# A hybrid encoder on one core: a q projection that ends token tile by token tile, gatings set apart, gate logits turned by full tiles

## The chip, the core and the metric

The kernel runs on one core of one Trainium2 chip. The metric is the device time of one execution in microseconds, of which the median of several runs is given. The engines named here are TensorE (PE; its weight loads are shown apart as PEld), VectorE (DVE), ScalarE (ACT), GpSimd (POOL) and SyncE (SP). Each takes its instructions in order. SyncE only issues DMAs here; GpSimd issues some too.

## The reference

Two layers, 256 tokens, model width 1024, everything in fp32. One input projection feeds two branches: a gated delta rule in both directions (in chunks of 64 tokens, after a convolution of width 5) and a differential softmax attention with partial rotary. Both have a SiLU gate path; they are merged with sigmoid gates.

```python
for l in range(DEPTH):
    h = rmsnorm(x, norm_w[l])
    proj = h @ w_in[l]
    (q_a, k_a, v_a, ab_a, z_a, q_b, k_b, v_b, z_b,
     gate_a, gate_b) = jnp.split(proj, SPLIT_IDX, axis=-1)
    y_a = gated_delta_branch(q_a, k_a, v_a, ab_a, z_a, conv_w[l], a_log[l], ...)
    lambda_init = 0.8 - 0.6 * math.exp(-0.3 * l)
    y_b = diff_attention_branch(q_b, k_b, v_b, z_b, cos, sin, diff_lambda[l], ...)
    merged = (jax.nn.sigmoid(gate_a) * (y_a @ w_pa[l])
              + jax.nn.sigmoid(gate_b) * (y_b @ w_pb[l]))
    x = x + merged @ w_out[l]
return rmsnorm(x, final_norm_w)
```

`ab_a` has 32 columns per token, the logits of the delta rule's gates. The attention's output is gated by the line `return o * jax.nn.silu(z)` at the end of its branch, `o` being a root-mean-square norm per head.

## The kernel before

**Tiles and products.** The 256 tokens are two token tiles of 128 (`m` = 0 and 1, NM = 2), the inner dimension is eight tiles of 128 (`kt`, KT = 8). Weights come from memory in pieces of 512 KB (`raw`, two inner tiles by 512 columns, called a `kp`), which ScalarE rounds to the upper part (`hi`, L308) and VectorE subtracts to the lower part (`lo`, L310). Each product is made of three: hi by hi, lo by hi, hi by lo (L324 to L326 in `proj_tm`, which accumulates one PSUM bank of 128 tokens by 512 columns for each token tile; L385 to L389 in the function for the convolution, with tiles pf_q, pf_k, pf_v and 256 columns). In a row of the profile lo_ga is then the lower part of a piece of the a gate's weights (`C_GA`, two halves of 512 columns, "ga0" and "ga1"), pp_ga its product; the b gate, gb, goes ahead of it. The rows leave out buffer numbers, so both token tiles' banks have one name there.

**What sets the order.** The program is written in the order of the data flow; a scheduler that simulates a time line decides each engine's order from it, from priorities, and from places written by hand: `behind(ins)` lets an instruction be issued only behind another one. `mark[name, kp]` keeps the instructions that made the upper and the lower part of a piece, so "after the lower part of ga0's third piece" is `mark["ga00", 2][1]` in the first layer. PSUM has eight banks in three pools; projections (pp, pf) take theirs in turn from one of four.

**The first place: q projection to v convolution.** The rotated attention's q comes in two halves; the second is "qk01" (evac_qk: ScalarE copies a token tile's bank to `stg`, L597, VectorE rotates, TensorE transposes). The first accumulator of the v convolution, pf_v, takes over the bank that token tile 0 of this projection leaves.

**The second: gate logits.** Their product abp has 64 rows: 32 columns of weights, upper and lower parts. It is copied to abT (64 x 256) and turned to tokens by rows by two products with id2, a 64 x 32 matrix of two identities above each other, which also adds the two parts (L636); VectorE copies the result to ab. Transposes of full tiles against the identity stand elsewhere, as ctk (L706). gcps (L764) is the first product that needs the logits.

**The third: gatings of the attention output.** For head half `i` and token tile `m`, VectorE multiplies the four heads by their factor and by the SiLU path (L1197, four instructions, ob), and transposes in blocks of 32 (L249, zb); GpSimd issues a DMA of 256 KB to a bounce buffer in memory (bny_yb, L251) and four DMAs of 64 KB that fetch it back turned (L257). `split_B` then makes the upper part on ScalarE (ybT, L263) and the lower one on VectorE (L265), for the product with w_pb. Around this stand the last steps of the delta rule's triangular inverse (`merges`, `join`): T, transposed blocks (L954); y128p and zt (L961); y1p and sp (L992), between which ScalarE copies A (L1000) and ktm (L1006); TensorE works through pp_ga between them. tb_q are squares for a norm of q (L135, L1046, L1047).

```python
at = [mark[f"ga{l}0", 1 + m][1] if i else mark[f"gb{l}1", 2 + m][1] for m in range(NM)]
```

This line of `gate_yb(i)` places the four gatings: half 0 behind the lower parts of the b gate's last two pieces, half 1 behind those of the a gate's second and third pieces.

Of the kernel before, what the change touches and what calls it, by code (L numbers as in the profile page):

```python
# [8 lines left out]
F32 = mybir.dt.float32  # L9
# [3 lines left out]
ALU = mybir.AluOpType  # L13
# [4 lines left out]
P = 128  # L18
DM = 1024
KT = DM // P  # L20
SEQ = 256
NM = SEQ // P
# [27 lines left out]
def hybrid_encoder(  # L50
# [44 lines left out]
    def bank_c(name):  # L95
        return ps_c.tile([P, 512], F32, tag="c", name=name)
# [4 lines left out]
    def last(ap, n):  # L101
        return ap.unsqueeze(ap.ndim).to_broadcast(list(ap.shape) + [n])

    mark = {}
# [4 lines left out]
    G.memset(ident, 1.0)  # L109
    G.affine_select(out=ident, in_=ident, compare_op=ALU.is_equal, fill=0.0,  # L110
                    base=0, pattern=[[1, P]], channel_multiplier=-1)
    id2 = const.tile([64, 32], F32, name="id2")
    V.tensor_tensor(id2, ident[0:64, 0:32], ident[0:64, 32:64], ALU.add)
    G.memset(tri, 1.0)
    for d, sg in ((0, 1), (1, -1)):
        G.affine_select(out=tri[:, d, :], in_=tri[:, d, :], compare_op=ALU.is_ge,
# [137 lines left out]
    def fetch(tb, dd, after):  # L254
        for j in range(4):
            with behind(after):
                G.dma_start(out=tb[blk(j)], in_=dd[:, :, j].rearrange("i t x -> t i x"))  # L257
# [55 lines left out]
                yield 2 * kp + k, hi[:, k, :n], lo[:, k, :n]  # L313

    def proj_tm(act, w, c0, n, evac, nm, places=(None,) * 4, spare=(), later=None, turned=(), between=None,
                banks=None, held=None, first=(), raws={}):

        accs = (banks or banks2)(f"pp_{nm}")
        for kt, hi, lo in weights(w, c0, n, nm, places, later=later, spare=spare, turned=turned, held=held,
                                  first=first, raws=raws):  # L320
            for m in range(NM):
                ts_ = slice(m * P, (m + 1) * P)
                o = accs[m][:, :n]
                T.matmul(o, act[kt // 4][:, 0, kt % 4, ts_], hi, start=kt == 0, stop=False)  # L324
                T.matmul(o, act[kt // 4][:, 0, kt % 4, ts_], lo, start=False, stop=False)  # L325
                mark["proj"] = T.matmul(o, act[kt // 4][:, 1, kt % 4, ts_], hi, start=False,  # L326
                                        stop=kt == KT - 1).ins
                mark["done", nm, kt] = mark["proj"]
        if between:
            between()  # L330
        for m in range(NM):
            evac(m, accs[m][:, :n])
# [174 lines left out]
    for l in range(DEPTH):  # L507
# [86 lines left out]
        def qk_part(s_, i):  # L594
                def evac_qk(m, ps):
                    st = work.tile([P, 512], F32, tag="w2a", name=f"stg{l}{s_}{i}{m}", bufs=2)
                    S.copy(st, ps)  # L597
                    g_ = st.rearrange("p (g e) -> p g e", e=DH)
                    x12 = g_[:, :, 0 : 2 * RD].rearrange("p g (x r) -> p g x r", x=2)
                    both = lambda t_: mid(mid(t_[:, m, :], 2), 8)  # L600
                    r4 = small.tile([P, 2, 8, 2, RD], F32, tag="r4", name=f"r4{l}{s_}{i}{m}", bufs=1)
                    V.tensor_tensor(r4[:, 0], x12, both(cos), ALU.mult)
                    V.tensor_tensor(r4[:, 1], x12, both(sin), ALU.mult)
                    V.tensor_tensor(x12[:, :, 0], r4[:, 0, :, 0], r4[:, 1, :, 1], ALU.subtract)
                    V.tensor_tensor(x12[:, :, 1], r4[:, 0, :, 1], r4[:, 1, :, 0], ALU.add)
                    pt = bank(f"qkt{l}{m}{s_}{i}")
                    for b in range(4):
                        T.transpose(pt[:, b * P : (b + 1) * P], st[:, b * P : (b + 1) * P], ident)

                    mark["qkT", m] = S.mul(qkT[i][:, s_, :, m * P : (m + 1) * P],  # L610
                                           pt.rearrange("p (b t) -> p b t", b=4), (DH ** -0.5, 1.0)[s_]).ins
                proj_tm(hT, wl, (C_QB, C_KB)[s_] + 512 * i, 512, evac_qk, f"qk{l}{s_}{i}",
                        turned=(0, 1) if (s_, i) == (0, 1) else ())

# [11 lines left out]
        for kt in range(KT):  # L628
            for part in range(2):
                T.matmul(abp[0:64, :SEQ], wabr[:, kt, :], hT[kt // 4][:, part, kt % 4, :],  # L630
                         start=kt == 0 and part == 0, stop=kt == KT - 1 and part == 1)
        abT = work.tile([64, SEQ], F32, tag="w2c", name=f"abT{l}", bufs=3)
        mark["ab"] = S.copy(abT, abp[0:64, :SEQ]).ins
        abq = bank_c(f"abq{l}")
        for m in range(NM):
            T.matmul(abq[:, m * 32 : (m + 1) * 32], abT[:, m * P : (m + 1) * P], id2,  # L636
                     start=True, stop=True)
        V.tensor_copy(ab.rearrange("p m c -> p (m c)"), abq[:, :64])

        a_ = small.tile([P, NM, 32], F32, tag="ga_", name=f"ga_{l}")  # L640
        V.tensor_scalar(a_[:, :, 0:16], ab[:, :, 0:16], -1.0, None, ALU.mult)
# [603 lines left out]
        V.scalar_tensor_tensor(rb, rb, 0.5 * (1.0 - lam0), r0, ALU.mult, ALU.mult)  # L1245

        ybT, yb_sent = pair(f"ybT{l}"), {}
        def gate_yb(i):
            at = [mark[f"ga{l}0", 1 + m][1] if i else mark[f"gb{l}1", 2 + m][1] for m in range(NM)]
            gated(lambda i, m: heads4(ob[i][:, m, :]), zb, rb, nw[:, 1:2], ybT, f"yb{l}",  # L1250
                  after={(i, m): at[m] for m in range(NM)}, halves_=(i,), sent=yb_sent)
            for m in range(NM):
                fetch(*yb_sent[i, m], None)

        gate_yb(0)
        gta = gate(C_GA, f"ga{l}", "eo", (lambda: gate_yb(1), None))
        for i, m in ((0, 0), (0, 1), (1, 0), (1, 1)):
            split_B(ybT[i], yb_sent[i, m][0], m, nw[:, 1:2], mark[f"ga{l}{i}", 2 + m])
        branch(ybT, w_pb[l], gtb, f"pb{l}")
# [137 lines left out]
```

## Time and profile before

| | |
|---|---|
| median of 3 runs | 743.0 us (742.79 to 744.36) |
| the profiled execution | 742.73 us |
| its span in the trace | 740.8 us |
| granted TensorE clock, mean | 0.997 of full |
| moved by DMA | 135.43 MB, mean 183 GB/s |

A row of the time line has the start and the length in microseconds, the engine, the line, the operation, the tiles it writes and reads, their shapes, and how many like instructions are taken together; in brackets stands how long the engine was idle ahead of it and what ended that. Matmuls are pipelined, so their lengths overlap, and the step from one start to the next is what one costs. A row of the view of waits has the engine and line that waited, what for, the sum in microseconds, the number of times and the longest. An fp32 product or transpose takes two passes and is counted twice.

### The profile page before, as it was taken

Reading aid. Unit: us, or ns where it says so; the run is one execution under the profiler, and the core shown is the slowest. Engines: PE = TensorE matmul, PEld = TensorE weight load, DVE = VectorE, ACT = ScalarE, POOL = GpSimd, SP = SyncE. Lnnn points to the kernel's source line nnn. Section 1 sums busy time; section 2 is a strip of 40 time slices with the busy share of each in tenths; the row PEclk is TensorE's granted clock in tenths of the full one; section 3 lists DMA queues with packets and bytes.
Section 4 is the critical chain, followed back from the end, with each engine's and each line's share of the span. In section 5 each row is a group of like instructions: output and inputs, shape, how many; then the busy total and the mean of one; then the engine's idle time right before and its main releaser. Section 6 shows DMA issues by size and latency. Waiting matters only on the chain.

```text
span 740.8 us, 13649 instructions
## 1 busy us (share of the span) xinstructions
PE 732.1 (99%) x5034; PEld 635.6 (86%) x5034; DVE 588.5 (79%) x1119; ACT 479.5 (65%) x1018; POOL 140.9 (19%) x223
## 2 busy tenths in 40 slices
PE   9999999999999999999999999999999999999996
PEld 6999889987888899888889899889788888998885
DVE  8696898999986885578667769999999769728782
ACT  6666875667876586645456578555787748665552
POOL 6004110112022433100000150202110514311000
PEclk9999999999999999999999999999999999999998
DMA  8755667776766473567674466767766736436641
GB/s 264 239 173 171 172 181 195 209 207 203 208 181 163 136 208 104 173 205 246 201 234 138 129 192 184 212 175 236 200 173 197 203 116 196 150 124 204 213 142 57
DMA packets 73732, 135.43 MB, mean 183 GB/s; under 512 B 12912, under 2 KB 13921, under 8 KB 73666
## 3 DMA queue, kind: packets, MB, share of 16 engines
q1 hardware_dynamic: 64750, 113.65, 51.6%
q0 software_dynamic: 7936, 19.35, 9.1%
q10 hardware_dynamic: 980, 1.58, 0.6%
q8 instruction: 39, 0.64, 0.4%
q14 instruction: 27, 0.22, 0.1%
HBM read 125.53 MB, written 9.01 MB: 182 GB/s over the span
## 4 chain that ended last, share of the span: by engine, by line
PE 96%; ACT 2%; issue 1%; DVE 1%; POOLq 0%; POOL 0%; DVEq 0%; ACTq 0%
PE pp_vb L369 4%; PE pp_qk L325 4%; PE pp_qk L326 3%; PE pp_qk L324 3%; PE sc L1067 2%; PE pp_o L369 2%; PE pp_za L325 2%; PE pf_k L385 2%; PE pf_v L385 2%; PE pf_v L389 2%; PE pp_ga L324 2%; PE pp_gb L324 2%; PE pp_zb L324 2%; PE pf_q L387 2%; PE pf_k L389 2%; PE pf_k L387 2%
## 5 line engine op out<-in xcount | busy, mean ns | idle before, releaser
L325 PE MATMUL pp_qk<-lo_qk,hT 128*128 128x512 f32 x128 | 50.5, 394 | 0.3
L326 PE MATMUL pp_qk<-hi_qk,hT 128*128 128x512 f32 x128 | 49.9, 390 | 0.0
L310 DVE TENSOR_TENSOR lo_qk<-raw_qk,hi_qk 128x1024 fp32r<-128x1024 f32 x32 | 39.1, 1221 | 12.0 <-ACT hi_qk L308 11.7
L324 PE MATMUL pp_qk<-hi_qk,hT 128*128 128x512 f32 x128 | 45.1, 393 | 0.0
L308 ACT CAST hi_qk<-raw_qk 128x1024 fp32r<-128x1024 f32 x28 | 29.4, 1049 | 23.4 <-PE pp_qk L326 12.7
L1077 ACT ACTIVATE es<-sc,mx 128x256 f32<-128x256 f32 x64 | 29.6, 473 | 19.5 <-DVE mx L1075 19.5
L385 PE MATMUL pf_q<-hT,hi_q 128*128 128x256 f32 x128 | 36.1, 285 | 0.0
L387 PE MATMUL pf_q<-hT,hi_q 128*128 128x256 f32 x128 | 35.9, 284 | 0.0
L385 PE MATMUL pf_k<-hT,hi_k 128*128 128x256 f32 x128 | 35.9, 286 | 0.0
L387 PE MATMUL pf_k<-hT,hi_k 128*128 128x256 f32 x128 | 35.9, 285 | 0.0
L385 PE MATMUL pf_v<-hT,hi_v 128*128 128x256 f32 x128 | 35.8, 285 | 0.0
L387 PE MATMUL pf_v<-hT,hi_v 128*128 128x256 f32 x128 | 35.8, 284 | 0.0
L389 PE MATMUL pf_q<-hT,lo_q 128*128 128x256 f32 x128 | 35.2, 288 | 0.0
L310 DVE TENSOR_TENSOR lo_pb<-raw_pb,hi_pb 128x1024 fp32r<-128x1024 f32 x16 | 19.6, 1225 | 18.9 <-ACT hi_pb L308 18.9
L389 PE MATMUL pf_v<-hT,lo_v 128*128 128x256 f32 x128 | 34.6, 288 | 0.0
L389 PE MATMUL pf_k<-hT,lo_k 128*128 128x256 f32 x128 | 34.3, 284 | 0.0
L308 ACT CAST hi_pa<-raw_pa 128x1024 fp32r<-128x1024 f32 x16 | 16.9, 1055 | 22.2 <-PE pp_pa L326 16.1
L679 DVE SCALAR_TENSOR_TENSOR cvq<-pf_q,cw,cvq 128x254 f32<-128x254 f32 (+1 forms) x64 | 30.0, 479 | 0.9 <-ACT cvq L675 0.4
L679 DVE SCALAR_TENSOR_TENSOR cvv<-pf_v,cw,cvv 128x254 f32<-128x254 f32 (+1 forms) x64 | 29.9, 479 | 0.1
L325 PEld LDWEIGHTS pp_qk<-lo_qk,hT 128*128 128x128 f32 x128 | 24.0, 188 | 6.6 <-DVE lo_qk L310 1.6
L679 DVE SCALAR_TENSOR_TENSOR cvk<-pf_k,cw,cvk 128x254 f32<-128x254 f32 (+1 forms) x64 | 28.5, 476 | 1.5 <-ACT cvk L675 0.9
L310 DVE TENSOR_TENSOR lo_pa<-raw_pa,hi_pa 128x1024 fp32r<-128x1024 f32 x16 | 19.6, 1224 | 11.2 <-ACT hi_pa L308 11.2
(416 smaller groups left out, 2535.1 us busy)
## 6 DMA issues: line engine op xcount, KB each, us to landing
raw_qk<-in_w_in_dram SPq DMA_DIRECT2D x32, 512.0 KB, 3.8
raw_k<-in_w_in_dram SPq DMA_DIRECT2D x16, 512.0 KB, 4.6
raw_q<-in_w_in_dram SPq DMA_DIRECT2D x16, 512.0 KB, 3.7
raw_v<-in_w_in_dram SPq DMA_DIRECT2D x16, 512.0 KB, 3.8
raw_zb<-in_w_in_dram SPq DMA_DIRECT2D x16, 512.0 KB, 4.0
raw_za<-in_w_in_dram SPq DMA_DIRECT2D x16, 512.0 KB, 3.8
raw_ga<-in_w_in_dram SPq DMA_DIRECT2D x16, 512.0 KB, 4.6
raw_pb<-in_w_pb_dram SPq DMA_DIRECT2D x16, 512.0 KB, 4.0
```

Of the source, the lines that this page charges most:

```text
L308: high = (V.tensor_copy if kp in turned else S.copy)(hi[:, :, :n], raw[:, :, :n]).ins
L310: mark[nm, kp] = high, V.tensor_tensor(lo[:, :, :n], raw[:, :, :n], hi[:, :, :n].bitcast(F32), ALU.subtract).ins
L324: T.matmul(o, act[kt // 4][:, 0, kt % 4, ts_], hi, start=kt == 0, stop=False)
L325: T.matmul(o, act[kt // 4][:, 0, kt % 4, ts_], lo, start=False, stop=False)
L326: mark["proj"] = T.matmul(o, act[kt // 4][:, 1, kt % 4, ts_], hi, start=False, stop=kt == KT - 1).ins
L369: mark["proj"] = T.matmul(o, act[kt // 4][:, pa, kt % 4, ts_], ws[kt][1 + pw], start=kt == 0 and n_ == 0, stop=kt == KT - 1 and n_ == 2).ins
L385: T.matmul(o, hi[:, cs], act[kt // 4][:, 0, kt % 4, :], start=first, stop=False, skip_group_check=True)
L387: T.matmul(o, hi[:, cs], act[kt // 4][:, 1, kt % 4, :], start=False, stop=False, skip_group_check=True)
L389: T.matmul(o, lo[:, cs], act[kt // 4][:, 0, kt % 4, :], start=False, stop=done, skip_group_check=True)
L679: V.scalar_tensor_tensor(ca[:, o0:o1], acc[:, b, o0 + sft : o1 + sft], cw[:, j, cb : cb + 1], ca[:, o0:o1], ALU.mult, ALU.add)
L1067: mm = T.matmul(sp[n][:, qt * SEQ : (qt + 1) * SEQ], qkT[h // 4][rows, 0, h % 4, qt * P : (qt + 1) * P], qkT[h // 4][rows, 1, h % 4, :], s ...
L1077: S.activation(es[:, n, qt, :], spv[:, qt, :], AF.Exp, bias=mx[:, n, qt : qt + 1], accum_out=s_all[:, h, n, qt : qt + 1])
```

## The change

Three edits. (1) `proj_tm` gets `by_tile`, used for "qk01" alone: the last two inner tiles are not multiplied as they come but held until both are there, and then first for token tile 0, then for token tile 1. (2) abT gets 128 rows, whose lower half GpSimd clears; the two products with id2 become two transposes of full 128x128 tiles, and VectorE adds the two halves behind its copy; id2 goes. (3) Each gating of the attention output has a place of its own: (0, 0) as before, (0, 1) behind the lower part of ga0's first piece, (1, 0) behind that of the third, (1, 1) behind that of the fourth. The places of the splits are not changed.

```diff
     def proj_tm(act, w, c0, n, evac, nm, places=(None,) * 4, spare=(), later=None, turned=(), between=None,
-                banks=None, held=None, first=(), raws={}):
+                banks=None, held=None, first=(), raws={}, by_tile=False):
 
         accs = (banks or banks2)(f"pp_{nm}")
+        ws = {}
         for kt, hi, lo in weights(w, c0, n, nm, places, later=later, spare=spare, turned=turned, held=held,
                                   first=first, raws=raws):
-            for m in range(NM):
+            ws[kt] = hi, lo
+            if by_tile and kt == KT - 2:
+                continue
+            todo = [(m, k) for m in range(NM) for k in ((kt - 1, kt) if by_tile and kt == KT - 1 else (kt,))]
+            for m, k in todo:
...
-                        turned=(0, 1) if (s_, i) == (0, 1) else ())
+                        turned=(0, 1) if (s_, i) == (0, 1) else (), by_tile=(s_, i) == (0, 1))
...
-        abT = work.tile([64, SEQ], F32, tag="w2c", name=f"abT{l}", bufs=3)
-        mark["ab"] = S.copy(abT, abp[0:64, :SEQ]).ins
-        abq = bank_c(f"abq{l}")
+        abT = work.tile([P, SEQ], F32, tag="w2c", name=f"abT{l}", bufs=3)
+        G.memset(abT[64:P], 0.0)
+        mark["ab"] = S.copy(abT[0:64], abp[0:64, :SEQ]).ins
+        abq = bank_c(f"abq{l}")[:, :SEQ].rearrange("p (m c) -> p m c", m=NM)
         for m in range(NM):
-            T.matmul(abq[:, m * 32 : (m + 1) * 32], abT[:, m * P : (m + 1) * P], id2,
-                     start=True, stop=True)
-        V.tensor_copy(ab.rearrange("p m c -> p (m c)"), abq[:, :64])
+            T.transpose(abq[:, m, :], abT[:, m * P : (m + 1) * P], ident)
+        V.tensor_copy(ab, abq[:, :, 0:32])
+        V.tensor_tensor(ab, ab, abq[:, :, 32:64], ALU.add)
...
-        def gate_yb(i):
-            at = [mark[f"ga{l}0", 1 + m][1] if i else mark[f"gb{l}1", 2 + m][1] for m in range(NM)]
+        def gate_yb(i, m, at):
             gated(lambda i, m: heads4(ob[i][:, m, :]), zb, rb, nw[:, 1:2], ybT, f"yb{l}",
-                  after={(i, m): at[m] for m in range(NM)}, halves_=(i,), sent=yb_sent)
-            for m in range(NM):
-                fetch(*yb_sent[i, m], None)
-
-        gate_yb(0)
-        gta = gate(C_GA, f"ga{l}", "eo", (lambda: gate_yb(1), None))
+                  (m,), {(i, m): at}, (i,), yb_sent)
+            fetch(*yb_sent[i, m], None)
+
+        def gate_others():
+            for i, m, kp, part in ((0, 1, 0, 1), (1, 0, 2, 1), (1, 1, 3, 1)):
+                gate_yb(i, m, mark[f"ga{l}0", kp][part])
+
+        gate_yb(0, 0, mark[f"gb{l}1", 2][1])
+        gta = gate(C_GA, f"ga{l}", "eo", (gate_others, None))
```

TensorE at the end of "qk01" in the first layer, before: pp_qk_1355 is the bank of token tile 0, pp_qk_1356 that of tile 1, the lines L324 to L326 are the three products, and the last row is the first of the v convolution.

```order
L324 MATMUL pp_qk_1356<-hi_qk_1411,hT_1_127 128x512
L325 MATMUL pp_qk_1355<-lo_qk_1412,hT_1_127 128x512
L326 MATMUL pp_qk_1355<-hi_qk_1411,hT_1_127 128x512
L325 MATMUL pp_qk_1356<-lo_qk_1412,hT_1_127 128x512
L326 MATMUL pp_qk_1356<-hi_qk_1411,hT_1_127 128x512
L324 MATMUL pp_qk_1355<-hi_qk_1411,hT_1_127 128x512
L325 MATMUL pp_qk_1355<-lo_qk_1412,hT_1_127 128x512
L326 MATMUL pp_qk_1355<-hi_qk_1411,hT_1_127 128x512
L324 MATMUL pp_qk_1356<-hi_qk_1411,hT_1_127 128x512
L325 MATMUL pp_qk_1356<-lo_qk_1412,hT_1_127 128x512
L326 MATMUL pp_qk_1356<-hi_qk_1411,hT_1_127 128x512
L385 MATMUL pf_v_1455<-hT_0_126,hi_v_1457 128x256
```

The same rows of the changed kernel, whose line numbers there are four higher:

```order
L328 MATMUL pp_qk_1356<-hi_qk_1411,hT_1_125 128x512
L329 MATMUL pp_qk_1355<-lo_qk_1412,hT_1_125 128x512
L330 MATMUL pp_qk_1355<-hi_qk_1411,hT_1_125 128x512
L328 MATMUL pp_qk_1355<-hi_qk_1411,hT_1_125 128x512
L329 MATMUL pp_qk_1355<-lo_qk_1412,hT_1_125 128x512
L330 MATMUL pp_qk_1355<-hi_qk_1411,hT_1_125 128x512
L329 MATMUL pp_qk_1356<-lo_qk_1412,hT_1_125 128x512
L330 MATMUL pp_qk_1356<-hi_qk_1411,hT_1_125 128x512
L328 MATMUL pp_qk_1356<-hi_qk_1411,hT_1_125 128x512
L329 MATMUL pp_qk_1356<-lo_qk_1412,hT_1_125 128x512
L330 MATMUL pp_qk_1356<-hi_qk_1411,hT_1_125 128x512
L389 MATMUL pf_v_1455<-hT_0_124,hi_v_1457 128x256
```

Token tile 0's last product has moved up from the eighth of these rows to the sixth; two products of tile 1 that stood ahead of it now stand behind, and one (the first row) is still ahead.

VectorE from the first gating of the attention output on, first layer, before: ob_0 and zb_0 are head half 0, ob_1 and zb_1 half 1, and x8 are both token tiles' gatings.

```order
L1197 SCALAR_TENSOR_TENSOR ob_0_383<-ob_0_383,rb_2862,zb_0_385 128x128 x8
L249 STREAM_TRANSPOSE zb_0_385<-ob_0_383 128x4x4x32 x2
L954 STREAM_TRANSPOSE T_2651<-U__96 32x8x32 x2
L954 STREAM_TRANSPOSE T_2658<-U__96 32x8x32 x2
L310 TENSOR_TENSOR lo_ga_2896<-raw_ga_2897,hi_ga_2895 128x1024
L1004 TENSOR_TENSOR ktm_360<-ktm_360,kds_372 128x512 x2
L310 TENSOR_TENSOR lo_ga_2914<-raw_ga_2915,hi_ga_2913 128x1024
L1004 TENSOR_TENSOR ktm_360<-ktm_360,kds_372 128x512 x2
L1197 SCALAR_TENSOR_TENSOR ob_1_384<-ob_1_384,rb_2862,zb_1_386 128x128 x4
L249 STREAM_TRANSPOSE zb_1_386<-ob_1_384 128x4x4x32
```

The changed kernel from the same gating on:

```order
L1202 SCALAR_TENSOR_TENSOR ob_0_383<-ob_0_383,rb_2862,zb_0_385 128x128 x4
L247 STREAM_TRANSPOSE zb_0_385<-ob_0_383 128x4x4x32
L959 STREAM_TRANSPOSE T_2651<-U__94 32x8x32 x2
L959 STREAM_TRANSPOSE T_2658<-U__94 32x8x32 x2
L308 TENSOR_TENSOR lo_ga_2885<-raw_ga_2886,hi_ga_2884 128x1024
L1009 TENSOR_TENSOR ktm_360<-ktm_360,kds_372 128x512 x2
L1202 SCALAR_TENSOR_TENSOR ob_0_383<-ob_0_383,rb_2862,zb_0_385 128x128 x4
L308 TENSOR_TENSOR lo_ga_2903<-raw_ga_2904,hi_ga_2902 128x1024
L1009 TENSOR_TENSOR ktm_360<-ktm_360,kds_372 128x512 x2
L247 STREAM_TRANSPOSE zb_0_385<-ob_0_383 128x4x4x32
```

Of the eight gatings of half 0 four stay, with one transpose; the other four stand behind the first lo_ga and its ktm, and their transpose (the last row) behind the second. Half 1 begins behind the third lo_ga, later than these rows.

ScalarE in the stretch of y1p and sp, first layer, before: hi_ga are upper parts of weights, the ybT row is the split of what token tile 1 of half 0 brought back, the copies of A are what the products sp read, and tb_q are the squares.

```order
L308 CAST hi_ga_2949<-raw_ga_2951 128x1024
L263 ACTIVATE ybT_0_2869<-zb_0_385,nw_308 128x4x128
L308 CAST hi_ga_2995<-raw_ga_2997 128x1024
L1000 COPY A_370<-y1p_3477 128x512
L1046 ACTIVATE tb_q_3455<-tb_q_3455 128x512
L1000 COPY A_370<-y1p_3489 128x512
L1046 ACTIVATE tb_q_3459<-tb_q_3459 128x512
L1046 ACTIVATE tb_q_3463<-tb_q_3463 128x512
L1000 COPY A_370<-y1p_3495 128x512
L1000 COPY A_370<-y1p_3483 128x512
```

The changed kernel at the same place:

```order
L306 CAST hi_ga_2938<-raw_ga_2940 128x1024
L306 CAST hi_ga_2995<-raw_ga_2997 128x1024
L261 ACTIVATE ybT_0_2869<-zb_0_385,nw_306 128x4x128
L1051 ACTIVATE tb_q_3455<-tb_q_3455 128x512
L1005 COPY A_370<-y1p_3477 128x512
L1005 COPY A_370<-y1p_3489 128x512
L1051 ACTIVATE tb_q_3459<-tb_q_3459 128x512
L1051 ACTIVATE tb_q_3463<-tb_q_3463 128x512
L1005 COPY A_370<-y1p_3495 128x512
L1005 COPY A_370<-y1p_3483 128x512
```

The split has moved behind the second hi_ga, next to the squares and the copies of A. On GpSimd the bounce of token tile 0 is now followed by its four fetches, then come tile 1's bounce and fetches; before, both bounces came first and then the eight fetches. On TensorE y1p keeps its place among the pp_ga, zt stands behind 14 of them and not 21, and sp, before in two pieces behind 6 and 12 of them, stands in one behind 13.

More of the change, by code (lines that the diff above doesn't have):

```diff
@@ L111, in hybrid_encoder @@
                     base=0, pattern=[[1, P]], channel_multiplier=-1)
-    id2 = const.tile([64, 32], F32, name="id2")
-    V.tensor_tensor(id2, ident[0:64, 0:32], ident[0:64, 32:64], ALU.add)
     G.memset(tri, 1.0)
@@ L315, in proj_tm @@
     def proj_tm(act, w, c0, n, evac, nm, places=(None,) * 4, spare=(), later=None, turned=(), between=None,
-                banks=None, held=None, first=(), raws={}):
+                banks=None, held=None, first=(), raws={}, by_tile=False):
         accs = (banks or banks2)(f"pp_{nm}")
+        ws = {}
         for kt, hi, lo in weights(w, c0, n, nm, places, later=later, spare=spare, turned=turned, held=held,
                                   first=first, raws=raws):
-            for m in range(NM):
+            ws[kt] = hi, lo
[3 more added lines that the diff above has]
+            for m, k in todo:
                 ts_ = slice(m * P, (m + 1) * P)
                 o = accs[m][:, :n]
[L324 to L328, printed above, removed]
+                hi, lo = ws[k]
+                T.matmul(o, act[k // 4][:, 0, k % 4, ts_], hi, start=k == 0, stop=False)
+                T.matmul(o, act[k // 4][:, 0, k % 4, ts_], lo, start=False, stop=False)
+                mark["proj"] = T.matmul(o, act[k // 4][:, 1, k % 4, ts_], hi, start=False,
+                                        stop=k == KT - 1).ins
+                mark["done", nm, k] = mark["proj"]
         if between:
```

## The prediction

> **What bounds the kernel now.** I read the head of the page first, then the chain that ended last, then the view of waits for TensorE's weight loads (PEld), because matmuls are issued in order and a wait shows first at the load in front of them.
>
> ```profile
> span 740.8 us, 13649 instructions
> PE 732.1 (99%) x5034; PEld 635.6 (86%) x5034; DVE 588.5 (79%) x1119; ACT 479.5 (65%) x1018; POOL 140.9 (19%) x223
> PE 96%; ACT 2%; issue 1%; DVE 1%; POOLq 0%; POOL 0%; DVEq 0%; ACTq 0%
> ...
> PEld pf_v L385 <- ACT stg L597: 0.8, 2, 0.4
> ```
>
> TensorE is busy for 732.1 of 740.8 us, and the chain that ended last runs 96% over it. So an edit counts in two ways only: it takes time out of TensorE's own stream, or it removes (or makes) a wait in that stream. VectorE, ScalarE and GpSimd matter only where TensorE stands still for them. The waits are small: the pf_v row is 0.8 us in 2 waits, one in each layer. I therefore look at the starts of neighbouring matmuls and not at their lengths, since the rows overlap (a 512-column matmul is shown as 0.39 us long below, and the next starts 0.23 later).
>
> **Part 1, the gate logits by full tiles.** Before, two narrow products (four rows, two passes each) stand in the middle of a convolution projection of 256-column matmuls. Elsewhere a pair of transposes of full tiles (ctk, 128x128 against the identity, the form that the new logits take) stands in the same kind of stream.
>
> ```profile
> 27.17 0.28 PE L389 MATMUL pf_k<-hT,lo_k 128*128 128x256 f32 x1
> 27.38 0.63 PE L636 MATMUL abq<-id,abT 64*128 64x32 f32 x4
> ...
> 28.16 0.28 PE L387 MATMUL pf_k<-hT,hi_k 128*128 128x256 f32 x1
> ```
>
> ```profile
> 45.50 0.28 PE L385 MATMUL pf_k<-hT,hi_k 128*128 128x256 f32 x1
> 45.62 0.38 PE L706 MATMUL ctk<-ident,kq 128*128 128x128 f32 x2
> ...
> 45.96 0.28 PE L389 MATMUL pf_k<-hT,lo_k 128*128 128x256 f32 x1
> ```
>
> From the start of the matmul ahead to the start of the second one behind it are 28.16 - 27.17 = 0.99 us with abq between, and 45.96 - 45.50 = 0.46 us with two transposes between. Two steps of 0.12 (45.50 to 45.62) would pass without either, so abq costs 0.75 and the pair 0.22. The place in the stream is kept: each layer gains 0.53 us, both together **1.06 us**. The bounds are the nearest rows again: nothing less than the pair's 0.22 is to be had, and at worst it costs its whole shown length and the longer gap ahead of abq (0.38 + 0.21 - 0.12 = 0.47), which leaves 0.28 a layer. I take the pair's row, which is the same operation in the same stream.
>
> The page "TensorE: Matmul & The Clock Gate" of the Trainium skill, section "Part 4: PE-mode transpose", speaks against this edit: it gives a 128x128 transpose about 275 ns inside a kernel. By that, an estimate, two would cost 0.55 us and a layer would gain 0.20; the ctk rows here do not agree with it as a price in the stream, 0.22 for the pair.
>
> Beside TensorE, GpSimd now clears the lower half of abT, and VectorE adds the two halves of the logits in one more instruction. I cost both at nothing.
>
> ```profile
> 27.82 0.18 POOL L768 MEMSET grow<- 128x96 f32 x1 [8.25 <-DVE lq L655]
> ...
> 39.20 0.52 PE L764 MATMUL gcps<-glog,tri 128*128 128x16 f32 x4
> ```
>
> GpSimd is idle for 8.25 us ahead of 27.82 and such a clearing takes it 0.2 us; the first matmul that needs the logits is at 39.20, 11 us behind abq, in which one more small VectorE operation (some 0.2 us, from the same row) is lost. Without that cover each would cost its 0.2 us. In the second layer the clearing stands on GpSimd behind the last bounce of the first layer's gatings and ahead of its four fetches, so it can hold them back; I give that no price of its own, since the split of what they bring is the last of four.
>
> **Part 2, the q projection that ends by token tile.** The bank of token tile 0 (pp_qk) is taken over by the first accumulator of the v convolution (pf_v), whose first matmul waits until ScalarE has copied the bank out (stg).
>
> ```profile
> 109.82 0.39 PE L324 MATMUL pp_qk<-hi_qk,hT 128*128 128x512 f32 x1
> ...
> 110.27 0.39 PE L326 MATMUL pp_qk<-hi_qk,hT 128*128 128x512 f32 x1
> ...
> 110.95 0.39 PE L326 MATMUL pp_qk<-hi_qk,hT 128*128 128x512 f32 x1
> 111.33 0.38 PE L385 MATMUL pf_v<-hT,hi_v 128*128 128x256 f32 x1
> 111.56 0.28 PE L387 MATMUL pf_v<-hT,hi_v 128*128 128x256 f32 x1
> ```
>
> ```profile
> 109.66 0.46 ACT L675 ACTIVATE cvq<-pf_q,cw 128x256 f32<-128x256 f32 x1
> 110.70 0.59 ACT L597 COPY stg<-pp_qk 128x512 f32<-128x512 f32 x1 [0.57 <-PE pp_qk L326]
> ```
>
> The last matmul of token tile 0 starts at 110.27; its copy starts 0.43 later, at 110.70, and ends at 111.29; pf_v starts 0.04 behind that. Undisturbed, pf_v would start one 512-column step (0.23, as 109.82 to 110.27 are two) behind 110.95 and its successor 0.12 later, at 111.30. It starts at 111.56, so 0.26 us are lost. In the order of the changed kernel, tile 0's last matmul moves up by only two places, to that of the row at 109.82. Its copy can then start at 109.82 + 0.43 = 110.25, just behind cvq on ScalarE (109.66 + 0.46 = 110.12), and end at 110.84, 0.3 us before pf_v wants the bank. The whole wait goes, 0.26 in each layer, **0.52 us**. Late next is nothing near: tile 1's copy waits for the same last matmul as before. Were the copy held up by more than 0.3 us, the gain would shrink one for one, at worst to nothing.
>
> **Part 3, the gatings of the attention output.** First what it frees. Ahead of the stage y128p, VectorE did both token tiles' gatings and transposes before it came to the four transposes T that y128p reads.
>
> ```profile
> 246.79 2.19 DVE L1197 SCALAR_TENSOR_TENSOR ob<-ob,rb,zb 128x128 f32<-128x128 f32 x8
> 248.90 1.99 DVE L249 STREAM_TRANSPOSE zb<-ob 128x512 f32<-128x512 f32 x2
> 250.92 1.84 DVE L954 STREAM_TRANSPOSE T<-U__96 32x256 f32<-32x256 f32 x4
> 252.79 1.23 DVE L310 TENSOR_TENSOR lo_ga<-raw_ga,hi_ga 128x1024 fp32r<-128x1024 f32 x1
> ...
> 259.61 1.23 DVE L310 TENSOR_TENSOR lo_ga<-raw_ga,hi_ga 128x1024 fp32r<-128x1024 f32 x1
> ```
>
> ```profile
> 252.22 0.68 PE L961 MATMUL y128p<-T,A 64*64 64x64 f32 x18
> ...
> 252.90 0.41 PE L961 MATMUL y128p<-T,A 64*64 64x64 f32 x7
> ...
> 252.22 1.79 PE L961 MATMUL y128p<-T,A 64*64 64x64 f32 x64
> ...
> 258.95 1.17 PE L961 MATMUL zt<-U__96,y 64*64 64x64 f32 x64
> ```
>
> T ends at 252.76. y128p, begun at 252.22, has 18 matmuls that end by 252.90, and goes on only there. Were the 18 steps even, the next would start some 0.04 us behind the eighteenth; the break stands right behind the end of the last T. I take 0.18 us of it for a wait, which goes, because with half of the gating moved behind them the T end some 2 us earlier by VectorE's rows (half of 2.19 and of 1.99), or as soon as ScalarE has their input: **0.36 us** in both layers. The bounds are nothing, if the break is the array's own, and 1.79 - 1.17 = 0.62 a layer, if y128p then runs as fast as zt, which has as many matmuls of that shape. I stay by the wait, near the lower end, since it alone has a cause in the rows.
>
> Then what it delays: the second tile's gating and transpose, and with them one exchange through memory (a bounce of 256 KB, bny_yb, then four fetches of 64 KB), whose result ScalarE splits for a product. ScalarE works in order, and this split stands ahead of the copies A that the matmuls sp need.
>
> ```profile
> 250.28 0.65 POOL L251 DMA_DIRECT2D bny_yb<-zb  x1 [3.73 <-DVE zb L249]
> ...
> 252.98 4.36 POOL L257 DMA_DIRECT2D zb<-bny_yb  x8 [1.25 <-DMA bny_yb<-zb]
> 260.08 0.56 POOL L251 DMA_DIRECT2D bny_yb<-zb  x1 [2.73 <-DMA wb_n<-in_norm_w_dram]
> 265.41 2.17 POOL L257 DMA_DIRECT2D zb<-bny_yb  x4 [4.77 <-DMA bny_yb<-zb]
> ...
> 633.41 2.17 POOL L257 DMA_DIRECT2D zb<-bny_yb  x4 [3.53 <-DMA bny_yb<-zb]
> ```
>
> ```profile
> DMA to landing us min/median/max: 2.2/4.2/4.7
> ...
> DMA to landing us min/median/max: 2.3/2.4/2.6
> ```
>
> The last two rows are those of the fetches at 265.41 and at 633.41, four each. When is the new result there? From the first lo_ga to the end of the second tile's transpose VectorE has the same set of work as it had from 252.79 to 259.61, 6.8 us, and starts it some 0.5 us earlier, so that the transpose ends at about 259.1 and the bounce is issued at 259.4 (0.3 to 0.4 behind it, as 250.28 behind the first half of 248.90 to 250.89). From a bounce to its first fetch are 2.70 us in one place (250.28 to 252.98) and 5.33 in another (260.08 to 265.41, behind eight fetches). The fourth fetch is issued 1.6 us behind the first, and lands 2.4 later in the quiet set and 4.2 in the other. So the last landing lies between 259.4 + 2.7 + 1.6 + 2.4 = 266.1 and 259.4 + 5.33 + 1.6 + 4.2 = 270.5.
>
> ```profile
> 264.35 1.27 ACT L263 ACTIVATE ybT<-zb,nw 128x512 fp32r<-128x512 f32 x1
> ...
> 266.44 0.59 ACT L1000 COPY A<-y1p 128x512 f32<-128x512 f32 x1
> ...
> 268.96 1.07 ACT L1000 COPY A<-y1p 128x512 f32<-128x512 f32 x2
> ...
> 270.80 2.84 PE L992 MATMUL sp<-A,ktm 128*128 128x128 f32 x24
> 273.39 0.48 PE L324 MATMUL pp_ga<-hi_ga,hT 128*128 128x512 f32 x1
> ```
>
> When is it needed? Behind y1p stood 12 pp_ga and 16 sp before 273.39, and now 13 and 16, so sp ends at about 273.4 as before; its third group of four starts two groups ahead of that, at 0.86 each (a third of 273.39 - 270.80, for 12 products of two passes): 271.7. ScalarE needs 1.27 for the split and then three squares and three copies A, 268.96 + 0.59 - 266.44 = 3.1 us in the same mixture. A landing after about 267.3 therefore stops TensorE, one for one. I take 266.6: ahead of this bounce now stand the first tile's four fetches and not eight, which puts it nearer to the quiet row. **Nothing is charged, with 0.7 us to spare.** Without them the price is up to 270.5 - 267.3 = 3.2 us a layer.
>
> The page "DMA: Bandwidth & Descriptors" of the Trainium skill, section "Anatomy of one DMA — SWDGE (gpsimd) path", gives 2.0 us and the bytes at 436 GB/s, by which the landing would be at about 265.8, an estimate. The row at 250.28 agrees with it, that at 260.08 does not.
>
> **The sum**, against the profiled execution (742.73 us, of which 740.8 are the span): 1.06 + 0.52 + 0.36 = 1.94, so 740.8 us. The median of the runs before, 743.0, is 0.27 above that execution; the forecast is 743.0 - 1.94 = **741.1 us**.
>
> **Rivals.** (A) The late split stops sp, and the kernel is slower. For it: the full row (5.33) and ScalarE's order; against it: the quiet rows. It decides from a landing at 267.3. At the bound it costs 3.2 us in each layer, 743.0 - 1.94 + 6.4 = 747.5; in one layer alone 744.3; a landing at 268.3 in both gives 743.1. (B) The pair of transposes costs 0.47 and the break in y128p stays: 743.0 - 0.56 - 0.52 = 741.9. The ctk rows speak against the first half. (C) Two places are too few and the projection's wait stays: 743.0 - 1.06 - 0.36 = 741.6. The 0.3 us to spare speak against it.
>
> **How the numbers follow.** Forecast 0.58, A 0.27, B 0.09, C 0.06. A measurement of this kernel tells about 0.2%, 1.5 us, from no change: faster is below 741.5, slower above 744.5. The forecast is faster; of A, 0.16 is slower and 0.11 within; B and C are within. So faster 0.58, same 0.26, slower 0.16. The range begins at 740.0 (y128p at its upper bound, 741.1 - 0.88 = 740.2, and a little for repeats) and ends at 744.5, which takes in A in one layer; left out is A in both, 0.16.
>
> **What would show it.** In the changed trace: an interval around the logits near 0.46; pf_v 0.23 behind the last pp_qk and no wait of it for stg; y128p without its break; a second ybT split that starts by 267.3. Wrong would be a wait of sp for ScalarE's A, which is A; a pf_v that still waits, which is C; or a new wait of lo_ga among the pp_ga, which nothing above foresees.

## The result, and the profile after

| | before | changed |
|---|---|---|
| median | 742.79 us (742.07 to 744.36, 7 runs) | 745.45 us (744.15 to 746.7, 7 runs) |
| the profiled execution | 742.73 us | 744.15 us |
| its span | 740.8 us | 742.3 us |
| ratio, with 95% interval | | 1.0034 [1.002, 1.0047] |

The changed kernel is slower, by 0.34%, about 2.5 us, where 741.1 us had been forecast. The profiled execution is the shortest of its seven, so what its rows show is the small side of the loss.

The head of the page of the changed kernel, and below it, from the view of waits for weight loads, the row that is new:

```profile
PE 731.6 (99%) x5030; PEld 635.4 (86%) x5030; DVE 589.5 (79%) x1120; ACT 479.5 (65%) x1018; POOL 139.3 (19%) x225
PE 86%; issue 4%; DMA 3%; ACT 3%; POOL 2%; DVE 2%; SPq 0%; POOLq 0%; DVEq 0%; ACTq 0%
...
PEld sp L997 <- ACT A L1005: 3.3, 4, 1.5
```

TensorE's own work is a little less than before (731.6 us for 732.1), but of the chain that ended last 14% now lie elsewhere than on TensorE, on DMAs, ScalarE and GpSimd among others, where 4% did. The row of pf_v waiting for stg is gone; in its stead sp waits for A, 3.3 us in four waits, in both layers.

The time line of TensorE in the changed kernel, at the gate logits, at the end of the q projection, and through y128p and zt:

```profile
26.93 0.29 PE L393 MATMUL pf_k<-hT,lo_k 128*128 128x256 f32 x1
27.05 0.38 PE L641 MATMUL abq<-ident,abT 128*128 128x128 f32 x2
...
27.39 0.29 PE L391 MATMUL pf_k<-hT,hi_k 128*128 128x256 f32 x1
...
110.20 0.39 PE L330 MATMUL pp_qk<-hi_qk,hT 128*128 128x512 f32 x1
110.43 0.28 PE L389 MATMUL pf_v<-hT,hi_v 128*128 128x256 f32 x1
110.54 0.28 PE L391 MATMUL pf_v<-hT,hi_v 128*128 128x256 f32 x1
...
251.33 1.48 PE L966 MATMUL y128p<-T,A 64*64 64x64 f32 x64
252.74 0.50 PE L328 MATMUL pp_ga<-hi_ga,hT 128*128 128x512 f32 x1
...
256.18 1.44 PE L966 MATMUL zt<-U__94,y 64*64 64x64 f32 x64
257.55 0.50 PE L329 MATMUL pp_ga<-lo_ga,hT 128*128 128x512 f32 x1
```

The first two parts of the change do what was worked out: 27.39 - 26.93 = 0.46 us around the logits (0.99 before), and pf_v's second matmul 0.34 us behind the last pp_qk (0.61 before). y128p has lost its break, 1.41 us to the next start and not 1.73. But zt, untouched by the diff, takes 1.37 where it took 1.10. The next starts behind y128p (252.22) and zt (258.95) in the kernel before:

```profile
253.95 0.50 PE L324 MATMUL pp_ga<-hi_ga,hT 128*128 128x512 f32 x1
...
260.05 0.50 PE L324 MATMUL pp_ga<-hi_ga,hT 128*128 128x512 f32 x1
```

The place of the loss, in the time lines of ScalarE, TensorE, GpSimd and SyncE of the changed kernel, and the landings of the four fetches at 262.88 and of the weight load at 263.41:

```profile
268.12 1.20 ACT L261 ACTIVATE ybT<-zb,nw 128x512 fp32r<-128x512 f32 x1 [4.19 <-DMA zb<-bny_yb]
...
269.75 1.05 ACT L1005 COPY A<-y1p 128x512 f32<-128x512 f32 x2
...
268.99 0.39 PE L328 MATMUL pp_ga<-hi_ga,hT 128*128 128x512 f32 x1
270.36 4.33 PE L997 MATMUL sp<-A,ktm 128*128 128x128 f32 x32 [0.98 <-ACT A L1005]
...
258.48 0.56 POOL L249 DMA_DIRECT2D bny_yb<-zb  x1 [5.20 <-DVE zb L247]
262.88 2.17 POOL L255 DMA_DIRECT2D zb<-bny_yb  x4 [3.85 <-DMA bny_yb<-zb]
...
263.41 0.37 SPq L302 DMA_DIRECT2D raw_ga<-in_w_in_dram  x1
...
DMA to landing us min/median/max: 2.2/3.7/4.2
...
DMA to landing us min/median/max: 4.0/4.0/4.0
```

Read from the bottom: the bounce is issued at 258.48 and its first fetch starts at 262.88, 4.4 us later. The first fetch lands 2.2 us after its issue, another 4.2 after, and ScalarE, idle for 4.19 us ahead of the split, starts it at 268.12. The squares and copies of A follow, and sp, whose turn comes 0.23 behind 268.99, starts at 270.36 and stops again inside (four of its products take 0.86 us, so 16 should take 3.5; they are shown as 4.33, of which some 0.25 is the length of the last). This is rival A of the prediction.

### The profile page after: what moved, and what is told of

It is laid out like the page before. It is cut to its first block, busy times and chain, and to the rows that moved or that the text cites. A ratio compares the mean times of both kernels' runs of the same rounds, so it can differ in the third digit from the quotient of the medians.

```text
span 742.3 us, 13644 instructions
## 1 busy us (share of the span) xinstructions
PE 731.6 (99%) x5030; PEld 635.4 (86%) x5030; DVE 589.5 (79%) x1120; ACT 479.5 (65%) x1018; POOL 139.3 (19%) x225
## 3 DMA queue, kind: packets, MB, share of 16 engines
q10 hardware_dynamic: 980, 1.58, 0.6%
## 4 chain that ended last, share of the span: by engine, by line
PE 86%; issue 4%; DMA 3%; ACT 3%; POOL 2%; DVE 2%; SPq 0%; POOLq 0%; DVEq 0%; ACTq 0%
PE pp_vb L373 4%; PE pp_qk L329 4%; PE pp_qk L330 3%; PE pp_qk L328 3%; PE sc L1072 2%; PE pp_o L373 2%; PE pp_za L329 2%; PE pf_k L389 2%; PE pp_zb L328 2%; PE pf_v L393 2%; PE pf_v L389 2%; PE pf_k L393 2%; PE pf_q L391 2%; PE pf_k L391 2%; PE pf_v L391 2%
```

## The experiments

Each is measured against runs of the kernel before on the same chip, whose medians were 742.6 to 742.7 us.

**e1: parts 1 and 2 alone.** The gatings as before.

```diff
-        def gate_yb(i, m, at):
+        def gate_yb(i):
+            at = [mark[f"ga{l}0", 1 + m][1] if i else mark[f"gb{l}1", 2 + m][1] for m in range(NM)]
...
```

> The changed kernel with the gatings placed as before (parts 1 and 2 alone). Theory S (the second ybT split waits for its fetches on ScalarE and holds back the A copies that sp reads; this is the whole loss): no PEld row of sp waiting for A, and 742.8 - 1.06 - 0.52 = 741.2 us. Theory P (parts 1 or 2 cost something that no row showed, such as the step by token tile): stays at 743 or above. If parts 1 and 2 bring what the rows promised, the steps in the trace are 0.46 us around the logits (0.99 before) and no wait of pf_v for stg.

Measured: 741.08 us against 742.62, ratio 0.9976 [0.9967, 0.9984]. No wait of sp and none of pf_v is left. The 1.58 us of parts 1 and 2 are there (1.54 between the medians), and theory P falls.

**e2: part 3 alone.** The kernel before with the changed `gate_yb`, `gate_others` and calls.

> The kernel before with the new places of the gatings alone (part 3). Theory S: sp waits for A in both layers, 1.6 us each or more, and the time is the changed kernel's plus what parts 1 and 2 bring, 745.4 + 1.6 = 747.0 us. Theory P: about 742.4, since part 3 would then only take the y128p break away.

Measured: 747.29 us, ratio 1.0059 [1.0044, 1.0073]. In its trace sp waits for A again:

```profile
PEld sp L992 <- ACT A L1000: 2.4, 3, 2.0
```

So part 3 costs 4.7 us by the medians; its profiled execution, 745.02 us, was the shortest of six, and its span is only 2.5 us above that of the kernel before (743.3 and 740.8). The wait was expected in both layers, 1.6 us or more in each; in this trace nearly all of it lies in the second. From the start of y1p to the first pp_pb the layers take 31.95 and 33.93 us, where the kernel before took 31.86 and 31.51. In the first layer all four fetches were issued ahead of the weight load that comes there (the last at 264.16, the load at 264.51). The parts add up: 4.7 - 1.5 = 3.2 beside the 2.5 to 2.7 measured for all three, within the runs' spread.

**e3: the second split behind A.** Everything of the change stays, but one place.

```diff
-            split_B(ybT[i], yb_sent[i, m][0], m, nw[:, 1:2], mark[f"ga{l}{i}", 2 + m])
+            split_B(ybT[i], yb_sent[i, m][0], m, nw[:, 1:2],
+                    mark[f"ga{l}1", 1] if (i, m) == (0, 1) else mark[f"ga{l}{i}", 2 + m])
```

> The changed kernel with the second split alone moved: behind the upper part of the second piece of ga1, so that it stands on ScalarE behind all four copies of A. Gatings, bounces and fetches stay as in the change. Theory S: no wait of sp, about 742.8 - 1.94 = 740.9 us, and no loss left. A rival (the exchange itself loads the DMA engines so that weights come late, or zt and sp in one piece cost TensorE more): the loss stays, 744 to 745.5 us, with other waits.

Measured: 740.91 us, ratio 0.9971 [0.9961, 0.9981]. In the time line of ScalarE the copies of A no longer stand behind the split (the last two of the four, then the split):

```profile
268.18 1.07 ACT L1005 COPY A<-y1p 128x512 f32<-128x512 f32 x2
...
271.79 1.24 ACT L261 ACTIVATE ybT<-zb,nw 128x512 fp32r<-128x512 f32 x1
```

One place on ScalarE takes the whole loss away, with the same exchange, at the same time, through memory. The view of waits has no row of sp. But e3 is not shown to be faster than e1: the 0.36 us that part 3 should add do not appear (740.91 and 741.08, intervals that overlap).

**e4: one weight load held back behind the fetches.** GpSimd writes one element in each of 32 rows of the load's buffer behind its four fetches, and the load must wait for that.

```diff
+                if nm[:2] == "ga" and nm[3:] == "1" and kp == 2:
+                    with behind(mark["fetch", 0, 1]):
+                        G.memset(raw[0:32, 0, 0:1], 0.0)
...
-            fetch(*yb_sent[i, m], None)
+            mark["fetch", i, m] = fetch(*yb_sent[i, m], None)
...
```

> The changed kernel with one weight load held back: the third piece of ga1 (issued at 263.41 in the changed kernel, 0.02 us ahead of the second fetch) waits for a one-element write by GpSimd that stands behind the four fetches of the second exchange. Theory D (a fetch issued behind a weight load lands only with it: 267.60 to 268.02 against the load's 267.39): the last fetch lands about 2.4 us after its issue, near 266.9 to 267.1 instead of 268.0, sp waits about 0.5 us a layer instead of 1.6, and the time falls by some 2 us, to about 743. If the landings are late for the exchange's own sake (its descriptors, or the bounce), they stay at 268 and so does the time, 745.4. The write by GpSimd adds 0.2 us there, off the path.

Measured: 742.3 us, ratio 0.9995 [0.9983, 1.0006]. By the medians 3 us are won back. By the two traces, counted from the start of the first large product (last section) to the end, it is 1.4 us (732.4 for 733.8). The time lines of GpSimd and SyncE, and the landings of those four fetches:

```profile
264.77 2.17 POOL L255 DMA_DIRECT2D zb<-bny_yb  x4 [3.85 <-DMA bny_yb<-zb]
...
267.49 0.12 POOL L296 MEMSET raw_ga<- 32x1 f32 x1
...
267.63 0.37 SPq L306 DMA_DIRECT2D raw_ga<-in_w_in_dram  x1
...
DMA to landing us min/median/max: 2.1/2.1/2.2
...
PEld sp L1001 <- ACT A L1009: 1.5, 4, 1.0
```

With the load behind them (267.63, not 0.02 us ahead of the second fetch) all four land 2.1 to 2.2 us after their issue, where they took up to 4.2. Theory D holds: a fetch issued just behind a 512 KB load lands just behind it. What is left of sp's wait, 1.5 us where 1.0 had been expected, belongs to what this edit does not touch: from the bounce to the first fetch 4.42 us pass here (260.35 to 264.77) and 4.40 in the changed kernel. (In this execution all of the first layer stands 1.9 us later than in the changed kernel's; the last section comes back to that.)

**e5: e3, with y128p and zt in turns.** Both stages' 64x64 products are chained, so that they keep the order in which they are written.

```diff
+                prev = mark["pin"]
                 for c, j4, g, d in every4:
-                    with behind(mark["pin"]):
-                        T.matmul(ps[g][halves[1 - row(d) if g == 0 else row(d)], c, j4, :],
+                    with behind(prev):
+                        prev = T.matmul(ps[g][halves[1 - row(d) if g == 0 else row(d)], c, j4, :],
...
```

> The kernel of e3 (the second split moved behind A) with the 64x64 products of y128p and zt held to the order in which they are written, two of one bank and two of the other in turn. In e3, as in the change, both stages run eight of one bank and eight of the other first, and each takes 1.37 to 1.41 us; zt of the kernel before, in turns of two, took 1.10. Theory Q (the order of the banks sets the pace): both take 1.1 us, 0.27 + 0.31 less in each layer, 740.9 - 1.16 = 739.8 us, less 0.1 to 0.2 a layer where pp_ga now breaks into zt, so 740.0. If the pace has another cause (weight loads, other traffic at that time), both stay at 1.4 and the time at 740.9.

Measured: 740.32 us, ratio 0.997 [0.996, 0.9981]; the lowest median of all here, but the interval overlaps that of e3, so the times do not show a gain on e3 (0.6 us between the medians). TensorE's time line:

```profile
250.85 1.16 PE L967 MATMUL y128p<-T,A 64*64 64x64 f32 x64
...
251.95 0.51 PE L328 MATMUL pp_ga<-hi_ga,hT 128*128 128x512 f32 x1
...
255.35 0.33 PE L967 MATMUL zt<-U__94,y 64*64 64x64 f32 x4
255.61 0.50 PE L329 MATMUL pp_ga<-lo_ga,hT 128*128 128x512 f32 x1
...
257.88 1.15 PE L967 MATMUL zt<-U__94,y 64*64 64x64 f32 x60
258.95 0.50 PE L330 MATMUL pp_ga<-hi_ga,hT 128*128 128x512 f32 x1
```

y128p takes 1.10 us and not 1.41: the order sets the pace, as theory Q has it. Zt's 60 passes take 1.07, but the four that stand apart take 0.26 and bring a second change of shapes with pp_ga, so most of zt's share is lost again.

**e6: e1, with the same order.** The gatings as before, y128p and zt in turns.

> The kernel of e1 (parts 1 and 2, gatings as before) with the same order of y128p and zt. Here y128p waits for the four T: by turns of two it needs the last T at its fourth product, so it should start or break off at once until T ends and then run 1.0 us: no gain in y128p, none in zt (which is in turns of two already), 741.1 us as e1, and e5 better by about 1 us. If the wait for T was never real, y128p takes 1.1 us here too and the time is 741.1 - 0.6 = 740.5.

Measured: 741.77 us, ratio 0.9985 [0.9977, 0.9994], 0.7 us above e1 by the medians. TensorE's time line of y128p:

```profile
251.47 0.47 PE L967 MATMUL y128p<-T,A 64*64 64x64 f32 x6
252.12 1.11 PE L967 MATMUL y128p<-T,A 64*64 64x64 f32 x58 [0.17 <-DVE T L959]
```

In this order the wait for T comes early, and the trace names it, so the wait that part 3 was to remove is real. From its start to the next product behind it (253.16) y128p takes 1.69 us here, 0.59 more than in e5, where T is early; in the order of eight and eight it takes 1.70 in e1, 0.29 more than in the changed kernel. That order hides half of the wait. The time was expected to be that of e1. The 0.7 us above it are not in y128p: zt breaks in two here (four passes at 258.13, the other 60 at 259.06), and from the start of y128p to that of y1p the first layer takes 11.75 us for 11.35 in e1.

**e7: the first exchange early.** The change, with only (0, 1) put back behind the b gate's last piece.

```diff
-            for i, m, kp, part in ((0, 1, 0, 1), (1, 0, 2, 1), (1, 1, 3, 1)):
+            for i, m, kp, part in ((1, 0, 2, 1), (1, 1, 3, 1)):
...
         gate_yb(0, 0, mark[f"gb{l}1", 2][1])
+        gate_yb(0, 1, mark[f"gb{l}1", 3][1])
```

> The changed kernel with the gating (0, 1) put back behind the b gate's last piece; (1, 0) and (1, 1) stay at their new, later places. Theory S: the loss hangs on (0, 1) alone; no wait of sp, 741.2 us as e1. If the later gatings of half 1 cost as well (their fetches, the clearing of abT ahead of them), the time is above e1's, up to 742.

Measured: 740.92 us, ratio 0.9978 [0.997, 0.9987], no wait of sp. The loss hangs on the gating (0, 1) alone; the other two later places cost nothing that can be told.

**e8: the changed kernel again**, a single run for a second trace.

> The changed kernel once more, for a second trace of the landings. Theory D: in each layer the last fetch lands 0.2 to 0.7 us behind the weight load that was issued around the first fetch, and sp waits one for one with it; with both waits larger than in the first trace (1.6 a layer) the time is nearer to 746, with equal ones 744.2.

Measured: 744.53 us; sp waits 3.4 us in four waits (3.3 in the first trace). In the first layer the load came ahead of the fourth fetch (263.90) and not of the second. Its row, then the landings of the first three fetches, then that of the fourth:

```profile
263.78 0.37 SPq L302 DMA_DIRECT2D raw_ga<-in_w_in_dram  x1
...
DMA to landing us min/median/max: 2.1/2.1/2.2
...
DMA to landing us min/median/max: 4.5/4.5/4.5
```

The three fetches ahead of the load take 2.1 to 2.2 us, the one 0.12 us behind it 4.5; it lands 0.2 us behind the load, and the last one of the second layer 0.4 behind its own. This is theory D again, with nothing held back by hand. Equal waits, and an equal time: so these two traces agree with 744.2 to 744.5, and the longer runs (up to 746.7) were not caught by a profile. Their excess can be a longer wait of the same kind (the runs of e2, with the wait, spread over 3.3 us, those of e3, without it, over 1.0), or an opening that takes 1.7 to 2.0 us longer, as in the traces of e4 and e7 (last section), which were among the longest of their runs. No trace decides it.

**e9: e5, with zt in one piece.** Zt begins with the bank whose input is copied last.

```diff
-            def quarters(ps, lhs, rhs, row):
+            def quarters(ps, lhs, rhs, row, turn=0):
...
                 for c, j4, g, d in every4:
+                    g, d = g ^ turn, d ^ turn
...
```

> The kernel of e5 with zt begun by the bank whose input is copied last, so that zt stays in one piece (behind 24 pp_ga); in e5 a first pair of zt stood 9 pp_ga ahead of the rest and the break cost 0.45 us a layer. By theory Q: y128p and zt 1.1 us each and unbroken, 740.3 - 0.9 = 739.4 us; but y1p now has one pp_ga after its first four products, which may cost 0.2 to 0.3 a layer, so 739.4 to 740.0. If ScalarE's copies of U (now behind one more hi_ga) come too late, y1p waits and the time is above 740.3.

Measured: 740.65 us, ratio 0.997 [0.996, 0.9981]: no better than e5, where 739.4 to 740.0 had been expected. Zt is whole, 258.47 to 259.56, but a new wait is there, and y1p is broken:

```profile
PEld pp_ga L329 <- DVE lo_ga L308: 1.0, 2, 0.5
...
258.47 1.16 PE L968 MATMUL zt<-U__94,y 64*64 64x64 f32 x64
259.56 0.50 PE L328 MATMUL pp_ga<-hi_ga,hT 128*128 128x512 f32 x1
...
262.88 1.05 PE L999 MATMUL y1p<-vtm,U__94 128*128 128x128 f32 x8
...
264.00 2.84 PE L999 MATMUL y1p<-vtm,U__94 128*128 128x128 f32 x24
```

With zt later, a pp_ga comes to need a lower part that VectorE has not made yet, 0.5 us in each layer. That alone is as much as the 0.9 us that were expected of the whole zt.

## Why the prediction was wrong

**The step that failed** is the landing in part 3: "I take 266.6 ... Nothing is charged, with 0.7 us to spare". The rest of that working held. TensorE came to this place 0.89 us earlier than before (y128p at 251.33 for 252.22), so the landing was needed by 267.3 - 0.9 = 266.4. The bounce was issued at 258.48, as worked out (259.4 - 0.9). From there to the first fetch it took 4.40 us, not near the 2.70 of the quiet row but nearer to the 5.33 of the full one; and from the first fetch to the split 5.24 us, again the full case (5.8) and not the quiet one (4.0). The split started at 268.12, 1.7 us too late, and TensorE lost those one for one. From the start of y1p to the first pp_pb it took 33.23 us in the first layer where e3, which differs in the place of the split alone, took 31.45 (rows below): 1.78 us more. Sp starts 1.14 us late (270.36 for 268.99 + 0.23) and loses some 0.6 inside. In the second layer the same stretch took 33.44 us for 31.48 in e3, 1.96 us more. (The kernel before took 31.86 and 31.51; why its first layer takes 0.4 us more than that of e3 was not looked into.)

Starts of y1p and of the first pp_pb, first the changed kernel, then e3 (the first product of its y1p):

```profile
262.69 3.73 PE L997 MATMUL y1p<-vtm,U__94 128*128 128x128 f32 x32
...
295.92 0.47 PE L328 MATMUL pp_pb<-hi_pb,ybT 128*128 128x512 f32 x1
```

```profile
263.24 0.27 PE L997 MATMUL y1p<-vtm,U__94 128*128 128x128 f32 x1
...
294.69 0.48 PE L328 MATMUL pp_pb<-hi_pb,ybT 128*128 128x512 f32 x1
```

**Why it was taken wrongly.** I put the choice between the two rows on how many fetches stood ahead of the bounce. The lateness has two parts. By the quiet rows the last landing would have been at 258.48 + 2.7 + 1.6 + 2.4 = 265.2; it was at 268.0. Of these 2.8 us, 1.7 lie between the bounce and its first fetch and 1.1 in the landing of the last fetch (3.5 us for 2.4). What decides the landings of the fetches is a weight load of SyncE's, as e4 and e8 show: 512 KB issued just ahead of them. The rows of the kernel before had it. SyncE's queue there, around the fetches at 265.41 (the full case) and at 633.41 (the quiet one):

```profile
265.73 0.37 SPq L304 DMA_DIRECT2D raw_ga<-in_w_in_dram  x1
...
631.51 0.37 SPq L304 DMA_DIRECT2D raw_ga<-in_w_in_dram  x1
636.84 0.37 SPq L304 DMA_DIRECT2D raw_pb<-in_w_pb_dram  x1
```

The full set has a load 0.3 us behind its first fetch and ahead of the other three, the quiet set has none between 631.5 and 636.8. I had read this queue in the first layer only, where four loads are taken together in one row, and did not set it beside GpSimd's. In the changed kernel the load at 263.41 is issued as soon as a lower part frees its buffer:

```profile
262.18 1.21 DVE L308 TENSOR_TENSOR lo_ga<-raw_ga,hi_ga 128x1024 fp32r<-128x1024 f32 x1
```

This one ends at 263.39. So loads follow the lower parts, and an exchange that is placed among these comes close to a load.

What makes the bounce slow is not shown. In the changed kernel and in e4 it lands 4.1 us after its issue, and a load is issued 0.8 us behind it (259.26 and 258.48). But in the second layer of e8 a bounce with a load as close behind it (621.87 and 622.65) lands after 2.4 us.

**Point by point.** Part 1 right, 0.53 us a layer. Part 2 right, 0.27 where 0.26 were worked out, and token tile 0's copy was early enough; rival C did not happen. Part 3's gain: the wait for T is real (e6) and y128p became 0.32 us shorter, between the 0.18 taken and the bound of 0.62. But zt became 0.27 longer, which no step of the prediction had: from the start of y128p to that of y1p the first layer takes 11.36 us before and after, so part 3 gains nothing there. The prediction put the changed order of TensorE at nothing and went by how many pp_ga stand between the stages, not by the order inside them. Rival A was right in place, mechanism and threshold, and got 0.27. Its price was bounded at 3.2 us a layer; part 3 cost 4.7 us in two layers (e2). The range, to 744.5, left out A in both layers, which is what happened: its two layers are not two draws, since the same schedule runs in both.

By the Trainium skill, page "DMA: Bandwidth & Descriptors", section "Anatomy of one DMA — SWDGE (gpsimd) path", a fetch of 64 KB would take about 2.15 us, an estimate from its 2.0 us and the bytes at 436 GB/s. The trace of e4 agrees (2.1 to 2.2, with no load just ahead); that of the changed kernel doesn't (up to 4.2 with one).

**What stays open.** In the second layer of the changed kernel and of e4 GpSimd stands still for 4.0 and 4.8 us ahead of the fetches, and the profile names nothing that released it, while the set of the first layer starts with its bounce's landing.

```profile
621.46 0.56 POOL L249 DMA_DIRECT2D bny_yb<-zb  x1 [4.96 <-DVE zb L247]
626.05 2.17 POOL L255 DMA_DIRECT2D zb<-bny_yb  x4 [4.03 <-issue]
```

The bounce at 621.46 lands after 2.8 us, and the first fetch starts 1.8 us behind that landing (0.3 in the first layer); the second layers of e2, e4 and e8 have the same 1.8 us. So the second layer is late by this stand and by the load at 626.51, ahead of its last three fetches, and not by a slow bounce. What holds GpSimd was not tried, nor what slows the bounce of the first layer, nor why some runs of the changed kernel are 2 us longer than both traces.

## What to carry to other kernels

A transfer that waits is dangerous by what stands behind its consumer on an engine that works in order: before moving work that feeds a DMA, list what is queued behind the instruction that takes the result, and give it the slowest landing that the trace has, not the likeliest. Look at all queues that issue transfers around it, weight loads above all. When a schedule shifts, read the order inside the stages that moved, not only their places. And where a late result is the only harm, moving the consumer is a cheap cure (e3); here it brought no more than undoing part 3 (e1), since that part had gained nothing by itself.

## What the hardware showed beside it

**The order of small products.** The 64 passes of a 64x64 stage take 1.10 us when two of one bank and two of the other come in turn, and 1.37 to 1.41 when eight of one bank come first, then eight of the other, and the remaining 16 in turns (e5 against e3 and the change, the same products and inputs). The program also places the two banks' products in different quarters of the array (`quarters`), so the runs do not tell whether the bank or the place in the array makes the difference. The orders of zt before and now:

```
L961 MATMUL zt12800_3417<-U__96,y12800_3380 64x64 x3
L961 MATMUL zt12801_3418<-U__96,y12801_3381 64x64 x2
L961 MATMUL zt12800_3417<-U__96,y12800_3380 64x64
L961 MATMUL zt12801_3418<-U__96,y12801_3381 64x64 x2
...
L966 MATMUL zt12800_3417<-U__94,y12800_3380 64x64 x8
L966 MATMUL zt12801_3418<-U__94,y12801_3381 64x64 x8
L966 MATMUL zt12800_3417<-U__94,y12800_3380 64x64 x2
...
```

**The opening varies by itself.** The first big projection started at 8.76 us in the kernel before and at 10.49 in e4, and at 8.53 in the changed kernel, whose TensorE order e4 shares. Its row in the kernel before, then in e4 (the first two of its six):

```profile
8.76 1.65 PE L464 MATMUL pp_vb<-wA_vb,hT 128*128 128x512 f32 x6 [0.24 <-ACT hT L234]
```

```profile
10.49 0.78 PE L472 MATMUL pp_vb<-wA_vb,hT 128*128 128x512 f32 x2
```

That is 1.7 us, as much as most effects here. The small products ahead of it, the same in number and order, take nearly twice as long in e4 (the eight passes of pt_h 1.91 us, 1.04 in the changed kernel); what makes them slow is not shown. Two executions should be compared from one landmark to the next, not by their ends.
